# Chunk recurrences of the RWKV-7 branch: two quarters in one walk instead of two walks

## The chip, the cores and the metric

The kernel runs on one NeuronCore of a Trainium2 chip. Its engines run side by side, each through its own queue in order: PE (TensorE: matmuls; PEld is its weight loads), DVE (VectorE), ACT (ScalarE), POOL (GpSimd) and SP, whose queue here issues nearly all DMAs. The metric is the device time of one launch in microseconds (us). Before the change the median of three runs is 1436.8 us (1435.89 to 1438.96).

## What is computed

Two decoder layers over 256 positions of width 1024, all in fp32. In each layer one wide input projection feeds three token mixers: A, a gated linear recurrence; B, a dilated attention; C, RWKV-7. Their outputs are projected, gated, summed and projected again; a layer norm, a SwiGLU feed-forward part with a short convolution and a second layer norm follow. Branch C has 16 heads of 64 channels, each with a 64 x 64 state, and is the part that the change touches. Cut to its core:

```python
def step(st, inp):                     # one position, all heads
    r_t, w_t, k_t, v_t, kk_t, a_t = inp
    sa = jnp.einsum('bhij,bhj->bhi', st, -kk_t)
    st = (st * w_t[:, :, None, :] + sa[..., None] * (kk_t * a_t)[:, :, None, :]
          + v_t[..., None] * k_t[:, :, None, :])
    return st, jnp.einsum('bhij,bhj->bhi', st, r_t)
_, y = lax.scan(step, zeros, xs)
y = group_norm(y) * ln_w + ln_b
y_c = (y + bonus) * (sigmoid(zg) @ g2)          # g2: low-rank factor of the gate, 128 x 1024
merged = g_a * (y_a @ proj_a) + g_b * (y_b @ proj_b) + g_c * (y_c @ proj_c)
```

## The kernel before

**Dense work.** Activations lie feature by position (128 features in the partitions, 256 positions along). An fp32 weight tile is split into a high part `whi` (ACT or POOL) and a rest `wlo` (DVE or POOL), activations likewise (`hh`, `hl`); three matmuls in the fast fp32 format then stand for one fp32 product (`mm3`, line 818). These matmuls, with `whi` or `wlo` in the name, are called dense here; they are a fixed list of jobs in a fixed order (`ORDER`, line 69: `z0` to `z3` make the inputs of the four quarters of branch C, `q` those of branch B, `x`, `e` those of branch A, `g` the merge gates, `b`, `a`, `c` the three output projections).

**Branch C.** `branch_c(qt)` (line 993) handles a quarter, four heads: two tiles of 128 partitions (index `j`) with two heads each (index `p`). It first prepares: decay, key norms, products within chunks of 64 positions (`KR`, `BK`, `AL`, `AR`), the inverse of a triangular 64 x 64 matrix per head and chunk (`inverse`, line 969: 15 steps of two POOL instructions on `VS`, then small matmuls `DN,Om`, `xq,Om`, `X,AL`, `XT,W` that end in `XT`). Then it walks through four chunks in order (from line 1216). A chunk has three steps, with a copy out of PSUM between them: the residual `R` (matmuls `St,KR` and `UV,AL`), the solve (`R,XT`, copied into `UV`), and the next state `St` (`UV,KB`) with the output `Y` (`AR,UV` and `KR,St`). The tail squares `Y`, sums over heads with two matmuls (`shi,blk` and `slo,blk`), takes a reciprocal root, multiplies by the gate (`zg,g`, which needs `g2`) and leaves `yc`. `yc_split` (line 1564) splits it into `ych`, `ycl`, the input of the last output projection, job `c`. Quarter 2 begins after quarter 0 has ended, quarter 3 after quarter 1.

**What sets the order.** The program is laid out by a planner, class `Flow` (line 77), when it is built. The dense jobs are one stream; the quarters, the two other branches and the splits are side streams, Python generators that give up control at `yield`. The planner keeps its own clock for each engine, and at each moment issues the step of a side stream whose inputs are ready by that clock, or else the next dense step. On the chip each engine then runs its list in order and waits where an input is late. In `group` (line 849), used for the first jobs of `c`, the planner emits matmuls on a tile of zeros (`idle`) for as long as its clock has the next input not ready:

```python
while k >= warm and ((*need, k) not in fl.done or fl.done[(*need, k)] > fl.t["PE"]):
    if spare is None:
        spare = faux()[:, :S]
    T.matmul(spare, idle[:, :128], idle, start=True, stop=True)
    yield
```

**Fetches.** `fetch` (line 370) puts a DMA on SP's queue. Weight tiles go through a ring of four; SP waits for the oldest to be used up, and what stands behind it in the queue waits too.

Of the kernel before, what the change touches and what calls it, by code (L numbers as in the profile page):

```python
# [24 lines left out]
F32 = mybir.dt.float32  # L25
# [8 lines left out]
S = 256  # L34
# [33 lines left out]
COOL = 5000  # L68
ORDER = "z0 q z1 z2 z3 g10 x0 x1 g11 e0 e1 b0 g00 g01 g21 b1 a0 g20 a1 c".split()
NC = 2  # L70
NB, NUP = (16, 24), 8

# [246 lines left out]
def hybrid_kernel(ctx: ExitStack, tc: tile.TileContext, x, c, positions, mod_w, w_in, w_qkv, w_vres, lru, lora, g2w,  # L319
# [571 lines left out]
    def layer(l):  # L891
# [101 lines left out]
        def branch_c(qt):  # L993
            ident, epsc = K["ident"], K["epsc"]
            if qt >= 2:
                yield ("C", l, qt - 2)
            vfs = []
# [5 lines left out]
            wa2 = LR[l][:, S * qt:S * qt + S]  # L1003
            g2 = t1([128, S], "g2")
            fetch(g2, g2w[l, :, S * qt:S * qt + S])
            if l:
# [39 lines left out]
            r_ = E["r", qt]  # L1046
            ce = sb.tile([128, 2, 4], F32, name="ce", bufs=4)
            V.tensor_copy(ce, cum[:, :, :, 64])
# [167 lines left out]
            Y = s2([128, 2, S], "Y")  # L1216
            Sp = None

            def bank():
                return aux().rearrange("p (j i) -> p j i", j=8)[:, :2]  # L1220

            for c_ in range(4):
                ps = bank()
                for p in range(2):
                    o = rows(1 - p)
                    for j in range(2):
                        if c_:
                            T.matmul(ps[o, j], KR[j][rows(p), c_, 0], Sp[rows(p), j], start=True, stop=False)
                        T.matmul(ps[o, j], AL[p][rows(p), c_, j], UV[p][rows(p), c_, j], start=not c_, stop=True)
                fl.sync()  # L1230
                R = t1([128, 2, 64], "R")
                SC.activation(R, ps, AF.Copy, scale=-1.0)
                yield
                ps = bank()
                for p in range(2):
                    o = rows(1 - p)
                    for j in range(2):
                        T.matmul(ps[o, j], XT[o, 2 * c_ + j], R[o, j], start=True, stop=True)
                fl.sync()
                V.tensor_copy(UV[0][rows(1), c_], ps[rows(1)])  # L1240
                SC.activation(UV[1][rows(0), c_], ps[rows(0)], AF.Copy)
                yield
                if c_ < 3:
                    ps = bank()
                    for p in range(2):
                        for j in range(2):
                            T.matmul(ps[rows(p), j], KB[p][:, j, c_], UV[p][:, c_, j], start=True, stop=True)
                    Sn = t1([128, 2, 64], "St")
                    if c_:
                        V.tensor_tensor(Sn, Sp, ce[:, :, c_:c_ + 1].to_broadcast([128, 2, 64]), OP.mult)  # L1250
# [7 lines left out]
                for p in range(2):  # L1258
                    for j in range(2):
                        T.matmul(psy[rows(p), j], UV[p][:, c_, j], AR[p][:, c_, j], start=j == 0, stop=not c_,  # L1260
                                 skip_group_check=True)
                if c_:
                    for j in range(2):
                        for p in range(2):
                            T.matmul(psy[rows(p), j], Sp[rows(p), j], KR[j][rows(p), c_, 1], start=False, stop=True,
                                     skip_group_check=True)
# [4 lines left out]
                yield  # L1271

            sq = s2([128, 512], "sq")
# [488 lines left out]
        def spawn_c(qt):  # L1762
            fl.spawn(("C", l, qt), branch_c(qt), 1)

# [11 lines left out]
        loras()  # L1776
        for z in ORDER:
            at.setdefault(z, len(jobs))
# [22 lines left out]
        n4 = len(jobs)  # L1801
        spread([(l, n) for n in range(NB[l], 40)], n1, n4)
# [4 lines left out]
        hook(n2 - 6, spawn_a)  # L1807
        hook(n3, m0_done)
# [135 lines left out]
```

## Time and profile before

| | |
|---|---|
| median of three runs | 1436.8 us |
| the profiled execution: time, span of its instructions | 1436.41 us, 1434.7 us |
| mean granted clock of PE | 0.975 |
| PE busy | 1331.7 us, 93% |
| DVE busy | 1118.9 us, 78% |
| ACT busy | 844.5 us, 59% |
| POOL busy | 280.3 us, 20% |
| DMA queues, share of 16 engines | 52% |

Busy time is the sum over an engine's instructions with overlaps counted once. PE's matmuls overlap, so the time of one in the trace (0.28 us for a dense one) is longer than the distance from one start to the next, and it is the distance that counts. The mixers of layer 0 lie between 122 and 474 us, those of layer 1 between 748 and 1172 us; job `c` follows at once.

### The profile page before, as it was taken

What the parts mean: (1) busy time and instruction counts of PE and PEld (TensorE: products, weight loads), DVE (VectorE), ACT (ScalarE), POOL (GpSimd) and SP (SyncE); (2) the same over time, 40 slices, a digit from 0 to 9 for tenths busy, and PEclk for the clock granted to TensorE, in tenths of its full rate; (3) what the DMA queues carried; (4) which work ended last, traced back from release to release, by engine and by line L of the source; (5) the groups of instructions that cost most, each with busy time, mean ns of one, the idle gap of its engine ahead of it and who ended that gap; (6) DMA issues with size and microseconds to landing.
All of it is one profiled execution on the core that took longest, in us unless ns stands there. A gap on an engine that the chain in (4) does not pass through costs nothing.

```text
span 1434.7 us, 32557 instructions
## 1 busy us (share of the span) xinstructions
PE 1331.7 (93%) x12786; PEld 1256.9 (88%) x12786; DVE 1118.9 (78%) x2559; ACT 844.5 (59%) x1744; POOL 280.3 (20%) x454
## 2 busy tenths in 40 slices
PE   4699999998989999999998999899989899999996
PEld 3689988887889999998988998888879799999996
DVE  7688769767875878999968757887598758799964
ACT  3556657567765556665456557565767445567643
POOL 1304034302420021000031402453204000420001
PEclk9889999999989999999999999999999999999999
DMA  8546426342554755778945542444335447367662
GB/s 301 196 160 192 153 87 214 100 140 76 197 170 138 233 176 177 256 246 297 328 145 181 157 156 98 147 143 137 117 106 175 148 134 234 98 230 233 213 190 69
DMA packets 77613, 249.21 MB, mean 174 GB/s; under 512 B 8754, under 2 KB 12082, under 8 KB 77460
## 3 DMA queue, kind: packets, MB, share of 16 engines
q1 hardware_dynamic: 76660, 244.62, 51.5%
q0 software_dynamic: 800, 2.52, 0.5%
q8 instruction: 100, 1.64, 0.5%
q14 instruction: 53, 0.43, 0.1%
HBM read 243.96 MB, written 3.15 MB: 172 GB/s over the span
## 4 chain that ended last, share of the span: by engine, by line
PE 60%; DVE 23%; ACT 8%; DMA 5%; issue 4%; SPq 0%; DVEq 0%; ACTq 0%
PE mm L267 45%; PE aux L267 9%; DVE wlo L267 7%; PE faux L267 6%; DVE u L267 2%; DMA w<-in_mod_w_dram 2%; ACT whi L267 2%; DVE w L267 1%; DVE wc L267 1%; DMA w<-in_w_in_dram 1%; DVE BK L267 1%; ACT L267 1%; DVE fal L267 1%; DVE xc L267 1%; ACT kk L267 1%
## 5 line engine op out<-in xcount | busy, mean ns | idle before, releaser
L267 ACT ACTIVATE whi<-w 128x512 fp32r<-128x512 f32 (+1 forms) x647 | 370.1, 617 | 230.3 <-PE mm L267 67.1
L267 PE MATMUL mm<-hh,whi 128*128 128x256 f32 x1704 | 500.8, 294 | 0.5 <-ACT ge L267 0.5
L267 PE MATMUL mm<-hh,wlo 128*128 128x256 f32 x1704 | 484.2, 284 | 14.1 <-DVE wlo L267 13.6
L267 PE MATMUL mm<-hl,whi 128*128 128x256 f32 x1704 | 481.9, 283 | 0.0
L267 DVE TENSOR_TENSOR wlo<-w,whi 128x512 fp32r<-128x512 f32 (+1 forms) x644 | 434.2, 705 | 56.5 <-ACT whi L267 53.7
L267 PEld LDWEIGHTS mm<-hh,wlo 128*128 128x128 f32 x1704 | 322.8, 189 | 17.7 <-DVE wlo L267 17.0
L267 PEld LDWEIGHTS mm<-hh,whi 128*128 128x128 f32 x1704 | 322.8, 189 | 13.4 <-issue 4.6
L267 PEld LDWEIGHTS mm<-hl,whi 128*128 128x128 f32 x1704 | 323.2, 190 | 0.9
L267 POOL TENSOR_TENSOR wlo<-w,whi 128x512 fp32r<-128x512 f32 x60 | 87.2, 1459 | 306.5 <-ACT whi L267 235.1
L267 POOL TENSOR_SCALAR whi<-w 128x512 fp32r<-128x512 f32 x57 | 40.8, 721 | 411.7 <-PE mm L267 272.5
L267 PE MATMUL mm<-fal,whi 128*128 128x256 f32 x352 | 99.1, 281 | 1.3 <-DVE fal L267 1.3
L267 PE MATMUL mm<-fah,wlo 128*128 128x256 f32 x352 | 99.2, 282 | 0.9 <-DVE wlo L267 0.8
L267 PE MATMUL mm<-fah,whi 128*128 128x256 f32 x352 | 99.3, 282 | 0.1
L267 DVE SCALAR_TENSOR_TENSOR u<-mm,par,u 128x255 f32<-128x255 f32 (+1 forms) x172 | 82.2, 479 | 12.9 <-ACT u L267 9.6
L267 PE MATMUL mm<-whi,hh 128*128 128x256 f32 x288 | 85.3, 296 | 0.0
L267 PE MATMUL mm<-wlo,hh 128*128 128x256 f32 x288 | 83.6, 290 | 1.2 <-DVE wlo L267 1.2
L267 PE MATMUL mm<-whi,hl 128*128 128x256 f32 x288 | 83.2, 289 | 0.0
L267 DVE SCALAR_TENSOR_TENSOR w<-w,s_bc 128x512 f32<-128x512 f32 x96 | 68.5, 739 | 0.1
L267 PEld LDWEIGHTS mm<-fah,wlo 128*128 128x128 f32 x352 | 66.4, 189 | 1.6 <-DVE wlo L267 1.5
L267 PEld LDWEIGHTS mm<-fal,whi 128*128 128x128 f32 x352 | 66.1, 188 | 1.6 <-DVE fal L267 1.5
L267 PEld LDWEIGHTS mm<-fah,whi 128*128 128x128 f32 x352 | 66.2, 188 | 0.3 <-ACT fah L267 0.3
L267 ACT ACTIVATE u<-mm,par 128x256 f32<-128x256 f32 x86 | 47.5, 554 | 23.1 <-PE mm L267 23.0
(438 smaller groups left out, 2729.8 us busy)
## 6 DMA issues: line engine op xcount, KB each, us to landing
w<-in_w_in_dram SPq DMA_DIRECT2D x132, 512.0 KB, 3.5
w<-in_w_up_dram SPq DMA_DIRECT2D x88, 512.0 KB, 3.9
w<-in_mod_w_dram SPq DMA_DIRECT2D x64, 512.0 KB, 4.4
w<-in_w_qkv_dram SPq DMA_DIRECT2D x36, 512.0 KB, 4.1
wc<-in_mod_w_dram SPq DMA_DIRECT2D x64, 256.0 KB, 4.7
w<-in_w_dn_dram SPq DMA_DIRECT2D x32, 512.0 KB, 4.4
w<-in_w_pa_dram SPq DMA_DIRECT2D x16, 512.0 KB, 3.9
w<-in_w_pc_dram SPq DMA_DIRECT2D x16, 512.0 KB, 3.8
```

The source lines that it names most:

```text
L267: r = f(*a, **k)
```

## The change

- A quarter's stream, now named `prep`, ends when `XT` is there. A new stream, `recurrence(pr)`, waits for the preparation of quarters `2*pr` and `2*pr + 1` and walks through the chunks for both: each step issues the matmuls of both (index `z`) into one PSUM bank; `R` and `St` become twice as wide and are copied once, while the copies into `UV` and `Y` stay one per quarter.
- The tail becomes a stream of its own, one per quarter; both start when the joint walk has ended. It fetches `g2` itself; before, the fetch stood at the start of the preparation.
- Quarters 2 and 3 still begin after the tails of 0 and 1.
- `ORDER` is given per layer, and `LATER`, `EARLY_A` and `FOLLOW` are new settings; at their values they change nothing.

```diff
+            E["cp", qt] = KR, AL, AR, UV, KB, XT
+            E["tail", qt] = k_
+        def recurrence(pr):
+            for z in range(2):
+                yield ("prep", l, 2 * pr + z)
+            Z = [E.pop(("cp", 2 * pr + z)) for z in range(2)]
...
+            each = [(p, z, j) for p in range(2) for z in range(2) for j in range(2)]
             for c_ in range(4):
                 ps = bank()
-                for p in range(2):
+                for p, z, j in each:
+                    KR, AL, AR, UV, KB, XT = Z[z]
                     o = rows(1 - p)
-                    for j in range(2):
-                        if c_:
-                            T.matmul(ps[o, j], KR[j][rows(p), c_, 0], Sp[rows(p), j], start=True, stop=False)
-                        T.matmul(ps[o, j], AL[p][rows(p), c_, j], UV[p][rows(p), c_, j], start=not c_, stop=True)
+                    if c_:
+                        T.matmul(ps[o, z, j], KR[j][rows(p), c_, 0], Sp[rows(p), z, j], start=True, stop=False)
+                    T.matmul(ps[o, z, j], AL[p][rows(p), c_, j], UV[p][rows(p), c_, j], start=not c_, stop=True)
                 fl.sync()
-                R = t1([128, 2, 64], "R")
+                R = t1([128, 2, 2, 64], "R")
...
-                SC.activation(Y[:, :, 64 * c_:64 * c_ + 64], psy, AF.Copy)
+                for z in range(2):
+                    SC.activation(Ys[z][:, :, 64 * c_:64 * c_ + 64], psy[:, z], AF.Copy)
...
+            for z in range(2):
+                fl.spawn(("C", l, 2 * pr + z), tail(2 * pr + z, Ys[z]), 1)
+        def tail(qt, Y):
+            g2 = t1([128, S], "g2")
+            fetch(g2, g2w[l, :, S * qt:S * qt + S])
...
-            fl.spawn(("C", l, qt), branch_c(qt), 1)
+            fl.spawn(("prep", l, qt), branch_c(qt), 1)
+            if qt % 2:
+                fl.spawn(("rec", l, qt // 2), recurrence(qt // 2), 1)
```

PE, layer 0, the residual step of the second chunk before: the step of one quarter (its tiles end in 725, 726, 883, 884, 1016, 1017), with `p = 0` in the first four rows and `p = 1` in the next four.

```order
L267 MATMUL aux<-St,KR_725 64x64
L267 MATMUL aux<-UV_883,AL_1016 64x64
L267 MATMUL aux<-St,KR_726 64x64
L267 MATMUL aux<-UV_883,AL_1016 64x64
L267 MATMUL aux<-St,KR_725 64x64
L267 MATMUL aux<-UV_884,AL_1017 64x64
L267 MATMUL aux<-St,KR_726 64x64
L267 MATMUL aux<-UV_884,AL_1017 64x64
```

The same step now, of which the first ten of sixteen rows stand here (the second quarter's tiles are 1987, 1988, 2172, 2303):

```order
L270 MATMUL aux<-St,KR_721 64x64
L270 MATMUL aux<-UV_879,AL_1012 64x64
L270 MATMUL aux<-St,KR_722 64x64
L270 MATMUL aux<-UV_879,AL_1012 64x64
L270 MATMUL aux<-St,KR_1987 64x64
L270 MATMUL aux<-UV_2172,AL_2303 64x64
L270 MATMUL aux<-St,KR_1988 64x64
L270 MATMUL aux<-UV_2172,AL_2303 64x64
L270 MATMUL aux<-St,KR_721 64x64
L270 MATMUL aux<-UV_880,AL_1013 64x64
```

The matmuls of `p = 0` of both quarters now come first, then those of `p = 1`; their number is the same.

PE, layer 1, where job `c` begins (`ych`: a quarter's split output; one job of the first three after the other, before):

```order
L267 MATMUL mm<-yah,wlo 128x256
L267 MATMUL mm<-ych,whi 128x256
L267 MATMUL mm<-ycl,whi 128x256
L267 MATMUL mm<-ych,wlo 128x256
L267 MATMUL mm<-ych,whi 128x256
L267 MATMUL mm<-ycl,whi 128x256
L267 MATMUL mm<-ych,wlo 128x256
L267 MATMUL faux<-ych,whi 128x256
L267 MATMUL faux<-ycl,whi 128x256
```

The same job now, after the inputs from quarters 0 and 1 are used up (the last residual step of quarters 2 and 3, tiles 13486 to 13941, stands right in it):

```order
L270 MATMUL faux<-ych,wlo 128x256
...
L270 MATMUL aux<-St,KR_13486 64x64
L270 MATMUL aux<-UV_13826,AL_13941 64x64
L270 MATMUL aux<-St,KR_13487 64x64
L270 MATMUL aux<-UV_13826,AL_13941 64x64
L270 LDWEIGHTS idle
L270 MATMUL faux<-idle 128x256
...
L270 MATMUL aux<-R,XT 64x64 x8
```

From there to the next `ych` row PE has 102 matmuls on the tile of zeros, and between them the last solve, the last output step and both tails; before, the job has none. In the whole program these matmuls go from 286 to 388. In layer 0 the job has none before and none now.

SP, layer 1, around the fetches of `g2` (`g`) for quarters 2 and 3 now (`w`: weight tiles, of job `c` and of the projection after it):

```order
L375 DMA w_15376<-in_w_pc_dram 128x1024
L375 DMA w_15419<-in_w_pc_dram 128x1024
L375 DMA g_15582<-in_g2w_dram 128x256
L375 DMA g_15590<-in_g2w_dram 128x256
L375 DMA w_15755<-in_w_o_dram 128x1024
```

Before, quarter 3's fetch stands some 40 rows earlier, among the weights of the input projection, beside its fetches of `v_first`. The change leaves the other counts nearly as they are: DVE has 16 instructions less, ACT 13 less (5 of them table loads), POOL 12 less, SP as many.

## Rows read from the trace of the kernel before

**Rows 1.** Page, share of the span by engine: busy, and the chain that ended last.
```profile
PE 1331.7 (93%) x12786; PEld 1256.9 (88%) x12786; DVE 1118.9 (78%) x2559; ACT 844.5 (59%) x1744; POOL 280.3 (20%) x454
...
PE 60%; DVE 23%; ACT 8%; DMA 5%; issue 4%; SPq 0%; DVEq 0%; ACTq 0%
```
**Rows 2.** Chain of waits, 1150 to 1200 us: start, length, what.
```profile
1149.85 0.39 PE aux L267 x8
...
1181.17 2.72 PE mm L267 x23
```
**Rows 3.** Waits of PE, 748 to 1172 us: us in total, times, longest.
```profile
PE aux L267 <- DVE DN L267: 4.4, 1, 4.4
...
PE aux L267 <- DVE UV L267: 0.3, 1, 0.3
```
**Rows 4.** Waits of PE, 122 to 474 us.
```profile
PE aux L267 <- DVE X L267: 3.2, 1, 3.2
...
PE aux L267 <- DVE DN L267: 0.4, 1, 0.4
```
**Rows 5.** PE in order of time, 518 to 531 us: start, length, instruction, count.
```profile
519.93 4.32 PE L267 MATMUL faux<-idle 128*128 128x256 bf16 x38
524.09 0.60 PE L267 MATMUL aux<-lsum,ones_d 128*128 128x256 f32 x2
```
**Rows 6.** PE in order of time, 280 to 283 us.
```profile
280.50 0.29 PE L267 MATMUL mm<-hh,wlo 128*128 128x256 f32 x1
280.72 0.32 PE L267 MATMUL aux<-St,KR 64*64 64x64 f32 x2
...
281.00 0.33 PE L267 MATMUL aux<-St,KR 64*64 64x64 f32 x4
...
281.40 0.28 PE L267 MATMUL aux<-UV,AL 64*64 64x64 f32 x2
281.61 0.39 PE L267 MATMUL mm<-hh,whi 128*128 128x256 f32 x1
```
**Rows 7.** PE in order of time, 1155 to 1156 us.
```profile
1155.33 0.28 PE L267 MATMUL mm<-hh,wlo 128*128 128x256 f32 x1
1155.54 0.46 PE L267 MATMUL aux<-R,XT 64*64 64x64 f32 x8
1155.92 0.39 PE L267 MATMUL mm<-hh,whi 128*128 128x256 f32 x1
```
**Rows 8.** ACT in order of time, the end of quarter 3, layer 1.
```profile
1154.38 0.28 ACT L267 ACTIVATE R<-aux 128x128 f32<-128x128 f32 x1 [1.34 <-PE aux L267]
...
1158.38 0.63 ACT L267 ACTIVATE sq<-Y 128x512 f32<-128x512 f32 x1
```
**Rows 9.** DVE in order of time, the same stretch.
```profile
1159.71 0.69 DVE L267 TENSOR_TENSOR slo<-sq,shi 128x512 fp32r<-128x512 f32 x1 [0.95 <-ACT shi L267]
...
1166.62 0.48 DVE L267 SCALAR_TENSOR_TENSOR yc<-sq,par,aux 128x256 f32<-128x256 f32 x1
...
1168.86 0.68 DVE L267 TENSOR_TENSOR ycl<-yc,ych 128x512 fp32r<-128x512 f32 x1
```
**Rows 10.** PE in order of time: the gate's matmuls, and where job `c` begins.
```profile
1164.19 1.02 PE L267 MATMUL aux<-zg,g 128*128 128x256 f32 x4
...
1172.49 0.28 PE L267 MATMUL mm<-ych,whi 128*128 128x256 f32 x1
```
**Rows 11.** DMA issues: KB each, median us from issue to landing.
```profile
g<-in_g2w_dram SPq DMA_DIRECT2D x8, 128.0 KB, 3.4
```
**Rows 12.** Waits of SP's queue: us in total, times, longest.
```profile
SPq L372 <- DVE wlo L267: 885.3, 282, 22.1
```
**Rows 13.** POOL in order of time: first and last row of quarter 3's inverse, layer 1.
```profile
1088.87 0.53 POOL L267 TENSOR_TENSOR itmp<-VS,N 128x15 f32<-128x15 f32 x1 [0.66 <-DVE N L267]
...
1114.31 0.23 POOL L267 TENSOR_TENSOR VS<-VS,itmp 128x8 f32<-128x8 f32 x1
```
**Rows 14.** PE in order of time, 1114 to 1123 us.
```profile
1122.59 1.08 PE L267 MATMUL aux<-DN,Om 32*32 32x32 f32 x64 [4.35 <-DVE DN L267]
```

More of the change, by code (lines that the diff above doesn't have):

```diff
@@ L68 @@
 COOL = 5000
-ORDER = "z0 q z1 z2 z3 g10 x0 x1 g11 e0 e1 b0 g00 g01 g21 b1 a0 g20 a1 c".split()
+ORDER = ["z0 q z1 z2 z3 g10 x0 x1 g11 e0 e1 b0 g00 g01 g21 b1 a0 g20 a1 c".split()] * 2
+LATER = ((0, 0), (0, 0))
+EARLY_A = (6, 6)
 NC = 2
+FOLLOW = "C"
 NB, NUP = (16, 24), 8
@@ L1046, in branch_c @@
             r_ = E["r", qt]
-            ce = sb.tile([128, 2, 4], F32, name="ce", bufs=4)
+            if qt % 2 == 0:
+                E["ce", qt // 2] = sb.tile([128, 2, 2, 4], F32, name="ce", bufs=4)
+            ce = E["ce", qt // 2][:, qt % 2]
             V.tensor_copy(ce, cum[:, :, :, 64])
@@ L1215, in branch_c @@
                 SC.activation(XT[r0:r0 + 32, :, 32:64], ps[r0:r0 + 32, :8], AF.Copy, scale=-1.0)
-            Y = s2([128, 2, S], "Y")
+            E["cp", qt] = KR, AL, AR, UV, KB, XT
[4 more added lines that the diff above has]
+            Z = [E.pop(("cp", 2 * pr + z)) for z in range(2)]
+            ce = E.pop(("ce", pr))
+            Ys = [s2([128, 2, S], "Y") for _ in range(2)]
             Sp = None
             def bank():
-                return aux().rearrange("p (j i) -> p j i", j=8)[:, :2]
+                return aux().rearrange("p (z j i) -> p z j i", z=4, j=2)[:, :2]
+            each = [(p, z, j) for p in range(2) for z in range(2) for j in range(2)]
             for c_ in range(4):
                 ps = bank()
-                for p in range(2):
+                for p, z, j in each:
+                    KR, AL, AR, UV, KB, XT = Z[z]
                     o = rows(1 - p)
-                    for j in range(2):
-                        if c_:
-                            T.matmul(ps[o, j], KR[j][rows(p), c_, 0], Sp[rows(p), j], start=True, stop=False)
-                        T.matmul(ps[o, j], AL[p][rows(p), c_, j], UV[p][rows(p), c_, j], start=not c_, stop=True)
+                    if c_:
+                        T.matmul(ps[o, z, j], KR[j][rows(p), c_, 0], Sp[rows(p), z, j], start=True, stop=False)
+                    T.matmul(ps[o, z, j], AL[p][rows(p), c_, j], UV[p][rows(p), c_, j], start=not c_, stop=True)
                 fl.sync()
-                R = t1([128, 2, 64], "R")
+                R = t1([128, 2, 2, 64], "R")
                 SC.activation(R, ps, AF.Copy, scale=-1.0)
@@ L1234, in branch_c @@
                 ps = bank()
-                for p in range(2):
+                for p, z, j in each:
                     o = rows(1 - p)
-                    for j in range(2):
-                        T.matmul(ps[o, j], XT[o, 2 * c_ + j], R[o, j], start=True, stop=True)
+                    T.matmul(ps[o, z, j], Z[z][5][o, 2 * c_ + j], R[o, z, j], start=True, stop=True)
                 fl.sync()
-                V.tensor_copy(UV[0][rows(1), c_], ps[rows(1)])
-                SC.activation(UV[1][rows(0), c_], ps[rows(0)], AF.Copy)
+                for z in range(2):
+                    UV = Z[z][3]
+                    V.tensor_copy(UV[0][rows(1), c_], ps[rows(1), z])
+                    SC.activation(UV[1][rows(0), c_], ps[rows(0), z], AF.Copy)
                 yield
@@ L1244, in branch_c @@
                     ps = bank()
[L1245 to L1248, printed above, removed]
+                    for p, z, j in each:
+                        UV, KB = Z[z][3:5]
+                        T.matmul(ps[rows(p), z, j], KB[p][:, j, c_], UV[p][:, c_, j], start=True, stop=True)
+                    Sn = t1([128, 2, 2, 64], "St")
                     if c_:
-                        V.tensor_tensor(Sn, Sp, ce[:, :, c_:c_ + 1].to_broadcast([128, 2, 64]), OP.mult)
+                        V.tensor_tensor(Sn, Sp, ce[:, :, :, c_:c_ + 1].to_broadcast([128, 2, 2, 64]), OP.mult)
                         fl.sync()
@@ L1257, in branch_c @@
                 psy = bank()
[L1258 to L1261, printed above, removed]
+                for p, z, j in each:
+                    UV, AR = Z[z][3], Z[z][2]
+                    T.matmul(psy[rows(p), z, j], UV[p][:, c_, j], AR[p][:, c_, j], start=z == j == 0, stop=not c_,
+                             skip_group_check=True)
                 if c_:
[L1263 to L1266, printed above, removed]
+                    for z in range(2):
+                        for j in range(2):
+                            for p in range(2):
+                                T.matmul(psy[rows(p), z, j], Sp[rows(p), z, j], Z[z][0][j][rows(p), c_, 1], start=False,
+                                         stop=True, skip_group_check=True)
                 fl.sync()
-                SC.activation(Y[:, :, 64 * c_:64 * c_ + 64], psy, AF.Copy)
+                for z in range(2):
+                    SC.activation(Ys[z][:, :, 64 * c_:64 * c_ + 64], psy[:, z], AF.Copy)
                 if c_ < 3:
@@ L1271, in branch_c @@
                 yield
+            for z in range(2):
+                fl.spawn(("C", l, 2 * pr + z), tail(2 * pr + z, Ys[z]), 1)
+        def tail(qt, Y):
+            epsc = K["epsc"]
+            k_ = E.pop(("tail", qt))
+            g2 = t1([128, S], "g2")
+            fetch(g2, g2w[l, :, S * qt:S * qt + S])
             sq = s2([128, 512], "sq")
@@ L1776, in layer @@
         loras()
-        for z in ORDER:
+        for z in ORDER[l]:
             at.setdefault(z, len(jobs))
@@ L1801, in layer @@
         n4 = len(jobs)
-        spread([(l, n) for n in range(NB[l], 40)], n1, n4)
+        spread([(l, n) for n in range(NB[l], 40)], n1 + LATER[l][0], n4 - LATER[l][1])
         load = out_proj()
@@ L1806, in layer @@
         hook(n1, spawn_b)
-        hook(n2 - 6, spawn_a)
+        hook(n2 - EARLY_A[l], spawn_a)
         hook(n3, m0_done)
```

4 lines of the change are left out of this document (1 added, 3 removed).

## The prediction

> **What bounds the kernel now.** I read the page first, then the chain of waits, the waits of PE in the two stretches of the mixers, and PE's instructions one by one where branch C's steps stand between dense matmuls. PE is busy for 93% of the span and holds 60% of the chain that ended last [rows 1]. Where branch C ends in layer 1 the chain is PE alone, matmul after matmul, from 1149.85 to 1183.9 us [rows 2]: whatever is put into PE's queue there moves the end by its own length. So the question is what the change adds to and takes from PE's list, and which waits of PE come or go.
>
> **The added idle matmuls.** The list of after has 102 more matmuls on the tile of zeros than before, all in job `c` of layer 1, before the inputs from quarters 2 and 3. They wait for nothing, so they take their time whether the inputs are early or late. 38 such matmuls in a row last from 519.93 to the next start at 524.09 us [rows 5]: 4.16 / 38 = 0.109 us each, and 102 x 0.109 = **+11.1 us**. Why they are there can be read from the order: before, quarter 2 of layer 1 began some 600 dense matmuls ahead of quarter 3 and was through long before job `c`; now both begin side by side, about where quarter 3 began, and share ACT, DVE and POOL up to the end. In layer 0 the last gate matmuls (`zg,g`) stand 61 rows of PE's list before the first of job `c`, against 64 before, and nothing is added.
>
> **The steps themselves.** The number of recurrence matmuls is unchanged; what changes is how they are packed. A residual step of one quarter: last dense start 280.50, first start of the step 280.72, of its second half (`p = 1`) 281.00, last start 281.40 in a row of two, so about 281.46, next dense 281.61 [rows 6]. A dense matmul takes 0.12 us from start to start, so going in costs 0.22 - 0.12 = 0.10 us and coming out about 0.15 - 0.06 = 0.09 us: 0.19 us for each interruption. Each matmul is two passes, and within one half they start 0.058 us apart (eight passes of the second half, 281.00 to 281.46). The first half would last 8 x 0.058 = 0.46 us, and the second begins 0.28 us after it: the halves overlap by three passes, 0.18 us.
>
> Doubled, the first half has 16 passes. If the overlap stays three passes, the second half starts after 13 x 0.058 = 0.75 us and ends 0.93 us later: 1.68 us, against 2 x (0.28 + 0.46) = 1.48 us: +0.20 us. The solve is the other case: all of it lies between 1155.33 and 1155.92 us [rows 7], 0.59 - 0.12 - 0.19 = 0.28 us, its halves of four passes nearly side by side; doubled, each half has eight as in rows 6, so 0.74 against 0.56: +0.18 us. I use +0.19 for all steps where the halves stand one behind the other. They are 15 in a joint walk (residual 4, solve 4, state 3, output 4), 60 in four walks: 60 x 0.19 = +11.4 us. Against that, the 96 steps of eight quarters become 48, and if each had interrupted the dense stream by itself, 48 x 0.19 = -9.1 us would be saved. But part of them shared an interruption already: by my count of the two lists the dense stream is interrupted 192 times in the two mixers before, 174 times after. But where steps shared one, a change of the tile's shape between them is saved, which costs about as much. I take both at two thirds, +7.6 - 6.1 = **+1.5 us**; the ends are -9 (no overlap lost) and +11 (nothing saved).
>
> The Trainium skill (TensorEngine Tiling (Array Packing), Key Properties) says that tiles operate independently and different ones can load weights and multiply in parallel. By that rule alone the halves would always run side by side; rows 6 show 0.28 us of delay in a step of eight passes a half, so here it holds for the last passes only. It gives one of the rivals below.
>
> **What leaves the other engines.** Sixteen ACT and sixteen DVE instructions and five table loads less, and some POOL work that the planner deals out anew. PE's work covers them all; where an engine in front of PE is late it shows in the waits below. I count nothing.
>
> **The end of both tails.** Before, the last walk takes from `R` at 1154.38 us [rows 8] to `ycl`, 1168.86 + 0.68 = 1169.5 us [rows 9]: 15.2 us, and the job that reads it starts at 1172.49 [rows 10], so 3 us before it would be needed. Now a second tail runs in the same stretch. On DVE, which is the slower of the two, that is 0.69 (`slo`), about as much for the product, 4 x 0.48 and 0.68 [rows 9]: about 4 us, to 19 us; on ACT five instructions of 0.63 as `sq` [rows 8] lie beside it. In PE's list the stretch from the last residual step on has 11.1 us of idle matmuls and some 4 us of the steps and sums (a solve 0.9, an output step 1.4, the sums and gates about 1.7, by the rows above), 15 us, and two more us are given by quarter 2's share of job `c`. So up to 19 - 17 = 2 us of real wait could stand behind the idle matmuls; less, since DVE has no dense work to prepare while PE idles. **+0.5 us**, between 0 and +4.
>
> **The fetch of `g2`.** It stood long before its use; now it is issued when the tail starts and read by `zg,g` at the tail's end, which is 1164.19 - 1158.38 = 5.8 us later in the walk of before [rows 8, 10]. It takes 3.4 us to land [rows 11], and two go one after the other. But SP's queue runs in order and waits a mean of 885.3 / 282 = 3.1 us for a weight tile's buffer [rows 12]; if the fetch stands behind such a wait it lands after 6.5 to 7 us, and PE, which takes `zg,g` in order, stops with all dense work behind it. The second tail lengthens the time until use by a few us. **+0.5 us**, between 0 and +5 (four pairs at a bit over 1 us).
>
> **The other waits.** PE waits for branch C's pieces (rows with `aux`) 8.8 us in layer 1 (eight rows, from 4.4 to 0.3) [rows 3] and 12.1 us in layer 0 (ten rows, from 3.2 to 0.4) [rows 4]. All of these places stand elsewhere in the new list. Half could vanish as well as half be added: 0, between -10 and +10.
>
> **Sum.** 11.1 + 1.5 + 0.5 + 0.5 = +13.6 on the profiled execution's 1436.41 us: 1450.0. The profiled execution lies 0.4 us under the median of the runs, which I leave. I trust the first term most and the packing least, and of the two ways in which the waits can go I see slightly more on the good side (half the walks, half the places to be late at), so I set **1448 us**, +11.6.
>
> **Rivals.**
> - *More waits at the inverses* (chance 0.15). Quarter 3's inverse in layer 1 took from 1088.87 to 1114.54 us on POOL among other work [rows 13], and PE then stood 4.35 us before `DN,Om` [rows 14]. Now two inverses of the second pair run at once in both layers, 60 instructions on the same queue. If PE stands that long at each of the four `DN,Om`, it is three more stops, 3 x 4.35 = 13 us: 1448 + 13 = 1461. Against it: the list puts these matmuls later than before, too.
> - *The walk's waits vanish and pay for the idle matmuls* (0.15). Half of the 20.9 us of `aux` waits gone is -10.4: 1438, no change.
> - *Faster* (0.10). The joint walk has half the round trips PE -> ACT -> PE, and with one walk instead of two there are fewer moments at which PE reaches a step before its copy. If nearly all `aux` waits vanish, -20.9, the result is 1448 - 20.9 = 1427. It turns faster from about 14 of the 21 us on. Against it: the largest of them, `DN` and `X`, stand before the walk, in the preparation.
> - *The halves overlap fully* (0.04). Then a doubled step lasts 0.93 us instead of 1.68, and the solve 0.46 instead of 0.74: about 0.3 us for the short ones and 0.75 for the 12 long residual steps, 48 x 0.28 + 12 x 0.75 = 22 us less: 1426. Rows 6 speak against it, and it is the rule named above.
>
> **Chances and range.** The forecast (1441 to 1456) has 0.56; with the first rival, slower is 0.71. No change (within 0.2%, 2.9 us, what a measurement of this kernel can tell) has 0.15, faster 0.14. The range reaches up into the first rival and down through no change: 1434 to 1460.
>
> **What will show it.** In the new profile: 388 idle matmuls, 102 of them in one stretch near 1170 us, about 11 us long, with little or no wait behind them; residual steps of about 1.9 us from dense to dense for two quarters; `zg,g` rows without a DMA as releaser. Wrong would be: PE reaching job `c` of layer 1 more than 5 us earlier than 1172.5 us (then waits did vanish), or more than 5 us later (then the second pair's preparation stopped it); or a solve step of two quarters well under 0.9 us.

## The result and the profile after

| | before | after |
|---|---|---|
| median, runs on one chip | 1436.35 us (1431.03 to 1438.96) | 1452.59 us (1449.85 to 1455.8) |
| profiled execution, span | 1436.41 us, 1434.7 us | 1455.8 us, 1454.1 us |
| mean granted clock of PE | 0.975 | 0.97 |

The change makes the kernel slower: ratio 1.0119, 95% interval [1.0083, 1.0155], +16 us. The forecast was 1448 us. The profiled execution of after lies 3.2 us above its median and has the lowest mean clock of the four: 0.970, where the other three have 0.976 and 0.977.

The page's busy times and chain, which answer to [rows 1]:

```profile
PE 1350.5 (93%) x12888; PEld 1282.8 (88%) x12888; DVE 1109.4 (76%) x2543; ACT 843.2 (58%) x1731; POOL 266.0 (18%) x442
...
PE 58%; DVE 21%; ACT 10%; DMA 6%; issue 4%; SPq 0%; POOL 0%; DVEq 0%; ACTq 0%
```

PE has its 102 matmuls more, DVE and ACT less work, and the share of ACT in the chain has grown. One place where ACT stands in it now and did not before [rows 2] is the end of the second pair in layer 1. PE in order of time there (start, length, instruction, count):

```profile
1172.81 0.28 PE L270 MATMUL faux<-ych,wlo 128*128 128x256 f32 x1
1173.02 0.32 PE L270 MATMUL aux<-St,KR 64*64 64x64 f32 x2
1173.18 0.28 PE L270 MATMUL aux<-UV,AL 64*64 64x64 f32 x2
1173.30 0.28 PE L270 MATMUL aux<-St,KR 64*64 64x64 f32 x2
...
1174.84 2.03 PE L270 MATMUL faux<-idle 128*128 128x256 bf16 x17
1176.80 0.96 PE L270 MATMUL aux<-R,XT 64*64 64x64 f32 x16
...
1178.57 0.97 PE L270 MATMUL aux<-AR,UV 128*64 128x64 f32 x16
...
1187.59 3.88 PE L270 MATMUL faux<-idle 128*128 128x256 bf16 x34
1191.22 0.36 PE L270 MATMUL mm<-ych,whi 128*128 128x256 f32 x1
1191.69 0.39 PE L270 MATMUL mm<-ycl,whi 128*128 128x256 f32 x1
```

The first row is a matmul of job `c`: PE reached this job at 1165.29 us, 7 us earlier than before [rows 10], because steps that stood ahead of it before now stand in it (about 10 us of small matmuls) and because PE waited 4.2 us less on the way there through layer 1. From 1174.84 to 1191.22 us, 16.4 us, there is no dense work: 11.1 us of matmuls on zeros (102 at 0.109 us) and 5.3 us of the last steps, sums and gates. What ended that stretch is told by the chain of waits (start, length, what):

```profile
1174.91 1.96 PE faux L270 x17
1176.87 0.89 PE aux L270 x16
1177.77 0.87 PE faux L270 x7
1178.64 1.53 PE aux L270 x32
1180.19 0.45 ACT Y L270 x2
...
1183.01 1.28 ACT L354
...
1190.55 0.48 DVE yc L270
1191.03 0.61 DVE ycl L270
1191.64 0.04 issue
1191.69 0.86 PE mm L270 x5
```

From 1180.19 us on it is the two tails, ACT and then DVE, and not PE's list as in [rows 2]. Ahead of that PE's list is in the chain: the 24 idle matmuls (`faux`) on both sides of the last solve hold it up for 2.8 us. The last `R` of the walk is copied at 1174.95 us, where before it was 1154.38 [rows 8]; from there to the last `ycl` it is 17.5 us, against 15.2.

Busy times in two stretches, of before and then of after (columns: stretch, its length, busy time and instructions of PE, PEld, DVE, ACT, POOL, mean granted clock of PE, DMA share, GB/s):

```profile
122.00:266.00 144.00, 135.73 (x1571) 125.56 (x1571) 115.00 (x297) 91.85 (x201) 39.43 (x75) 0.96 0.47 154
266.00:360.00 94.00, 86.51 (x1005) 77.84 (x1005) 66.52 (x140) 60.50 (x127) 13.28 (x26) 0.98 0.33 107
```
```profile
122.00:266.00 144.00, 141.46 (x1733) 132.99 (x1731) 102.38 (x259) 84.64 (x194) 32.92 (x53) 1.00 0.48 158
266.00:360.00 94.00, 76.53 (x525) 70.13 (x523) 76.27 (x158) 65.37 (x123) 17.77 (x22) 0.87 0.33 111
```

In layer 0 after is first ahead, then loses more than it gained: while the first pair's tails and the second pair's preparation run, PE is idle for 17.5 us of 94 (7.5 before) and the clock granted is 0.87 in the mean: 2.4 GHz but for five pieces at 1.2 GHz, 23.9 us together, each of which begins in or right behind a stop of PE of 1.1 to 2.6 us. What PE waits for there in after (us in total, times, longest):

```profile
PE mm L270 <- DVE wlo L270: 5.5, 3, 2.6
PE aux L270 <- DVE yc L270: 3.1, 2, 1.6
PE aux L270 <- ACT shi L270: 2.8, 2, 1.6
PE mm L270 <- ACT whi L270: 2.2, 1, 2.2
```

In before the same stretch has 4.6 us on `wlo` and nothing else over 0.6.

**Where the 16 us are.** I count from start to start on PE, between dense matmuls that both kernels have (those with `ehi` and `elo` in the name, of job `e`, counted in; the 500th to the 2420th are layer 0's mixers, S0; the 4300th to the 6690th layer 1's mixers and job `c`, S1). S0 goes from 371.7 to 379.6 us: waits +4.5, dense matmuls at the lower clock +3.1, the rest +0.3. S1 goes from 446.4 to 456.2: idle matmuls +11.1, small matmuls +3.5, waits -4.1, lower clock +2.4, and the dense matmuls -3.1, which stays unexplained. After S1 the profiled execution loses 4.5 more and between the mixers 0.9; it had started 3.7 us ahead. Together that is its +19.4.

Of layer 0's part the waits come back and the clock does not. The lists of PE in layer 0 are the same in after and in three of the kernels below (no_idle, rec_l1, g2_early). Their S0 is 377.0 to 378.2 us, with waits of 27.2 to 28.2 us against 22.1 before, and the lower clock costs their dense matmuls no more than in before (7.3 to 7.5 us each, 10.6 in after): in the second stretch above their mean clock is 0.92 to 0.95, but in the first 1.00, where before has 0.98 and 0.96. So the 3.1 us of clock belong to this one execution; a loss of 5 to 8 us, with waits of 4.5 to 6, is what the change does to layer 0.

### The profile page after: what moved, and what is told of

Read it like the earlier page. It is cut to its first block, busy times and chain, and to the rows that moved or that the text cites. A ratio compares the mean times of both kernels' runs of the same rounds, so it can differ in the third digit from the quotient of the medians.

```text
span 1454.1 us, 32738 instructions
## 1 busy us (share of the span) xinstructions
PE 1350.5 (93%) x12888; PEld 1282.8 (88%) x12888; DVE 1109.4 (76%) x2543; ACT 843.2 (58%) x1731; POOL 266.0 (18%) x442
## 4 chain that ended last, share of the span: by engine, by line
PE 58%; DVE 21%; ACT 10%; DMA 6%; issue 4%; SPq 0%; POOL 0%; DVEq 0%; ACTq 0%
PE mm L270 43%; PE aux L270 9%; DVE wlo L270 7%; PE faux L270 6%; ACT whi L270 2%; DVE u L270 2%; DMA w<-in_w_in_dram 2%; DMA w<-in_mod_w_dram 2%; DVE wc L270 1%; DVE w L270 1%; DVE BK L270 1%; ACT L270 1%; DVE xc L270 1%; DVE sq L270 1%; ACT kk L270 1%
## 5 line engine op out<-in xcount | busy, mean ns | idle before, releaser
L270 ACT ACTIVATE whi<-w 128x512 fp32r<-128x512 f32 (+2 forms) x655 | 374.0, 616 | 221.6 <-PE mm L270 65.9
L270 PE MATMUL mm<-hl,whi 128*128 128x256 f32 x1704 | 487.0, 286 | 0.0
L270 DVE TENSOR_TENSOR wlo<-w,whi 128x512 fp32r<-128x512 f32 (+1 forms) x648 | 435.8, 704 | 59.7 <-ACT whi L270 58.3
L270 PEld LDWEIGHTS mm<-hh,wlo 128*128 128x128 f32 x1704 | 330.9, 194 | 19.1 <-DVE wlo L270 18.7
L270 PEld LDWEIGHTS mm<-hh,whi 128*128 128x128 f32 x1704 | 331.6, 195 | 17.0 <-issue 6.7
L270 PEld LDWEIGHTS mm<-hl,whi 128*128 128x128 f32 x1704 | 331.5, 195 | 1.2
L270 POOL TENSOR_TENSOR wlo<-w,whi 128x512 fp32r<-128x512 f32 x56 | 77.8, 1397 | 307.9 <-ACT whi L270 187.7
L270 POOL TENSOR_SCALAR whi<-w 128x512 fp32r<-128x512 f32 x49 | 34.3, 707 | 475.3 <-PE mm L270 354.6
```

The costliest lines, as they stand in the source:

```text
L270: r = f(*a, **k)
```

## The experiments

The table has what the trace of each kernel gives by the same count; the medians of before were 1435.6, 1436.9 and 1437.1 us beside them. "Small" is all non-dense, non-idle matmuls of S0 and S1, "waits" PE's gaps there, "idle" the matmuls on zeros in job `c`. "Walk" is the part of "small" that the walk's own matmuls take, with time in stretches at 1.2 GHz counted half: an estimate of their price at full clock, from the granted clock of each trace. Every row is one execution, so "small" and S0, S1 also hold what the clock did in it; "walk" is 68.9 to 69.1 us in all five kernels whose joint walk goes in blocks.

| kernel | median us | ratio to before, 95% interval | S0 | S1 | small | walk | waits | idle |
|---|---|---|---|---|---|---|---|---|
| before | 1436.4 | | 371.7 | 446.4 | 205.9 | 67.0 | 51.3 | 0 |
| after | 1452.6 | 1.0119 [1.0083, 1.0155] | 379.6 | 456.2 | 209.8 | 69.0 | 51.7 | 11.1 |
| no_idle | 1452.2 | 1.0105 [1.0075, 1.0135] | 378.2 | 456.2 | 213.7 | 69.1 | 61.7 | 0 |
| rec_l1 | 1457.7 | 1.0138 [1.0106, 1.0170] | 377.0 | 462.5 | 211.6 | 68.9 | 62.2 | 0 |
| b_coupled | 1439.3 | 1.0022 [1.0000, 1.0043] | 371.3 | 449.9 | 208.4 | 66.1 | 43.3 | 12.4 |
| pair_split | 1446.0 | 1.0060 [1.0040, 1.0080] | 374.9 | 453.6 | 198.4 | 58.8 | 63.8 | 0 |
| stagger | 1445.8 | 1.0060 [1.0040, 1.0080] | 372.8 | 453.8 | 202.1 | 69.0 | 46.5 | 13.6 |
| g2_early | 1455.3 | 1.0132 [1.0096, 1.0169] | 377.7 | 461.2 | 208.3 | 68.9 | 57.0 | 8.3 |
| b_p_inner | 1424.0 | 0.9905 [0.9878, 0.9932] | 368.9 | 438.3 | 195.9 | 58.7 | 46.2 | 0 |
| p_inner | 1419.5 | 0.9872 [0.9840, 0.9904] | 362.7 | 440.8 | 189.2 | 49.7 | 46.7 | 5.0 |
| b_p_inner2 | 1408.8 | 0.9796 [0.9769, 0.9824] | 361.2 | 426.4 | 191.9 | 61.2 | 42.8 | 0 |
| p_inner2 | 1410.1 | 0.9814 [0.9779, 0.9848] | 357.4 | 435.8 | 181.5 | 49.6 | 45.5 | 5.0 |
| p2_stagger | 1416.3 | 0.9864 [0.9822, 0.9907] | 360.1 | 436.7 | 177.1 | 49.5 | 46.1 | 11.4 |
| ps2 | 1434.0 | 0.9985 [0.9966, 1.0004] | 361.4 | 452.1 | 188.6 | 53.2 | 49.5 | 16.3 |

**1. Are the idle matmuls the price? (no_idle)** In `group` the planner waits for the input of `c` where it put idle matmuls:

```diff
-                while k >= warm and (... fl.done[(*need, k)] > fl.t["PE"]):
+                if need[0] == "yck" and (... fl.done[(*need, k)] > fl.t["PE"]):
+                    yield (*need, k)
+                while need[0] != "yck" and k >= warm and (...):
```

> The changed kernel without its 102 idle matmuls in job c of layer 1; the planner waits there instead. Theory A (the end of branch C is late and the idle matmuls only fill the time until then): the time stays at 1452 us (1449 to 1456); PE stands about 11 us before the rows of quarter 2's input, which are ready near 1191 us in the trace of the changed kernel. Theory B (the idle matmuls cost their own length, as the prediction has it): 1452.6 - 11.1 = 1441.5 us.

The time is that of after, as theory A has it. PE now waits, as its rows in order of time show (idle time and releaser in brackets):

```profile
1179.67 0.80 PE L270 MATMUL aux<-shi,blk 128*128 128x512 f32 x1 [1.72 <-ACT shi L270]
...
1186.93 0.38 PE L270 MATMUL mm<-ych,whi 128*128 128x256 f32 x1 [1.21 <-ACT ych L270]
...
1189.48 0.58 PE L270 MATMUL mm<-ycl,whi 128*128 128x256 f32 x1 [2.17 <-DVE ycl L270]
```

From 1174 to 1186 us the granted clock is 0.57 here and 1.00 in the same place of after: PE, which stands still in between, falls to 1.2 GHz, its small matmuls take up to twice as long (16 `AR,UV` 1.76 us for 0.97), and still the end is no later. From the copy of `Y` to the end of the chain in `ycl` ACT and DVE take 11.45 us in both traces (1177.99 to 1189.44 us here, 1180.19 to 1191.64 in after; the chain's rows here follow). Ahead of it the 2.8 us of idle matmuls in the chain are gone, but the slower matmuls take all but 0.6 us of them back. So most of the idle matmuls fill a stretch that the late tails make, and taking them out wins nothing. Two things change together here, the matmuls on zeros and the clock; no run separates them.

```profile
1177.99 0.45 ACT Y L270 x2
...
1188.83 0.61 DVE ycl L270
1189.44 0.04 issue
```

**2. What does the pairing of starts and ends cost by itself? (b_coupled)** Before, with its separate walks; in layer 1 quarters 2 and 3 both wait for both of the first pair (and two buffers are dealt out otherwise, 24 and 45 for 21 and 46, so that it fits).

```diff
                 yield ("C", l, qt - 2)
+                if l:
+                    yield ("C", l, 3 - qt)
```

> The kernel before the change, every quarter with a walk of its own, but in layer 1 quarters 2 and 3 both wait until both of the first pair have ended (two pool sizes changed to make room: 24 small buffers for 21, 45 large for 46). PE's list has 113 idle matmuls in job c of layer 1. Theory A (starting as a pair is what makes the end late): 12 to 16 us over the kernel before, 1448 to 1453 us. Theory B (walking together is what costs): within 3 us of the kernel before, 1434 to 1440 us.

It has 12.4 us of idle matmuls in job `c` (113, where after has 102) and costs 3 us (0 to 6 by the interval), the time of theory B: the waits elsewhere in layer 1 went down by 7.8 us. The wait for `DN` [rows 14] is among those gone, as it is in after. A late end in layer 1 is therefore no loss of its full length.

**3. The second pair earlier (rec_l1).** After, where in layer 1 the second pair begins when the first joint walk has ended, not the tails.

```diff
-                yield (FOLLOW, l, 0) if FOLLOW == "rec" else (FOLLOW, l, qt - 2)
+                yield ("rec", l, 0) if l else ("C", l, qt - 2)
```

> The changed kernel, but in layer 1 quarters 2 and 3 begin when the joint walk of the first pair has ended, not after its tails. PE's list then has 286 idle matmuls as before the change, none of them in job c. Theory A (what costs in layer 1 is that the second pair starts late, as a pair): the stretch of idle matmuls goes, 11 to 16 us less, 1437 to 1442 us, and the 4 to 5 us lost in layer 0 stay. Theory B (the joint walk itself costs): little change, 1448 us or more.

No idle matmul is left in job `c`, and the kernel is no faster than after. Theory A missed by more than 15 us; theory B's bound of 1448 held, though not its "little change": the median is 5 us above after's, with intervals that overlap. PE's waits rose to 62 us; the longest new one, 4.1 us, is for `slo` of a tail. I take it that work moved earlier to relieve the end came to lie beside the first pair's tails; no run shows that apart.

**4. The steps without sharing (pair_split).** After's pairing, but a bank, an `R` and an `St` for each quarter, one quarter's matmuls after the other's.

```diff
-                ps = bank()
-                for p, z, j in each:
+                for z in range(2):
+                    ps = bank()
+                    for p, j in each:
...
-                SC.activation(R, ps, AF.Copy, scale=-1.0)
+                    SC.activation(R[z], pss[z], AF.Copy, scale=-1.0)
```

> The changed kernel with its pairing kept (both preparations first, the two quarters step by step in one stream, both tails after it, the next pair after the tails), but each quarter with banks, R and St of its own as before the change. PE's list has no idle matmuls in job c. Theory A (the pairing costs: two tails and two preparations fall together, the dense work's wlo comes late and PE's clock falls): near the changed kernel, 1446 to 1455 us. Theory B (the shared banks and double-width copies cost): back near the kernel before, 1435 to 1441 us.

Its small matmuls take 198.4 us, 7.5 less than before and 11.4 less than after; the walk at full clock takes 8.3 less than before and 10.2 less than after. A residual step of two quarters costs 1.557 us beyond a dense matmul (1.916 in after), a solve 0.749 (0.982). These are the two opposite terms of the packing: pairing saves the entry and exit, and joint steps with the halves in blocks lose the overlap. The edit changes banks, copies and order at once; what the order does alone, experiment 5 shows. The time, 1446.0 us, is at the lower edge of theory A's range all the same: what the steps and the missing idle matmuls save is taken back by 12.1 us more of waits and by the lowest granted clock of all these kernels (0.966 in the trace).

**5. Halves in turn (b_p_inner, p_inner).** The loops are turned round, so that matmuls of `p = 0` and `p = 1` alternate; nothing else changes. In before (b_p_inner; the solve, state and output likewise) and in after (p_inner):

```diff
-                for p in range(2):
-                    o = rows(1 - p)
-                    for j in range(2):
+                for j in range(2):
+                    for p in range(2):
+                        o = rows(1 - p)
```
```diff
-            each = [(p, z, j) for p in range(2) for z in range(2) for j in range(2)]
+            each = [(p, z, j) for z in range(2) for j in range(2) for p in range(2)]
```

> The kernel before the change with the two halves (p) of a step issued in turn, matmul by matmul, instead of one half after the other. Theory A (the array runs the halves side by side whenever the list lets it, so what the prediction priced at 0.28 us of delay per step is a matter of the order): a residual step falls from 1.11 us dense to dense to about 0.85, the other steps by 0 to 0.2; 8 x (3 x 0.28 + 8 x 0.1) = 13 us at most on PE's list, of which waits take some back: 1423 to 1432 us. Theory B (the array takes the second half late whatever the order): no change, 1434 to 1439 us.

> The changed kernel with the halves (p) of a step issued in turn. In the kernel before, this took a residual step from 0.98 to 0.75 us beyond the dense matmul; doubled steps have twice as many passes to lay side by side: residual 1.92 to about 1.2, solve 0.98 to 0.75, state and output 2.17 to about 1.7. Per joint walk 3 x 0.7 + 4 x 0.23 + 4 x 0.45 = 4.8 us, four walks 19 us. Theory A (these are PE time on the chain): 1452.6 - 19 = 1433 us (1428 to 1438), and steps of these lengths. Theory B (doubled steps overlap no better): 1448 to 1453 us.

Both became faster than before, b_p_inner as its theory A has it, p_inner 8.5 us below the range of its theory A (1428 to 1438). The residual step in p_inner, in order of time; in after it is the first group of rows above:

```profile
426.90 0.28 PE L270 MATMUL mm<-yah,wlo 128*128 128x256 f32 x1
427.11 0.34 PE L270 MATMUL aux<-St,KR 64*64 64x64 f32 x4
427.27 0.29 PE L270 MATMUL aux<-UV,AL 64*64 64x64 f32 x4
427.39 0.33 PE L270 MATMUL aux<-St,KR 64*64 64x64 f32 x4
...
427.97 0.33 PE L270 MATMUL aux<-UV,AL 64*64 64x64 f32 x4
428.23 0.39 PE L270 MATMUL mm<-yah,whi 128*128 128x256 f32 x1
```

From the dense matmul ahead to the matmul behind it is 1.33 us instead of 2.03 in after (1172.81 to 1174.84). Rows of four now start 0.12 us apart, where in after rows of two do: the halves run side by side. For one quarter, in b_p_inner, it is 0.87 us from 972.76 us to 973.63 instead of 1.11 [rows 6]:

```profile
972.76 0.28 PE L267 MATMUL mm<-hh,wlo 128*128 128x256 f32 x1
972.97 0.34 PE L267 MATMUL aux<-St,KR 64*64 64x64 f32 x4
...
973.63 0.39 PE L267 MATMUL mm<-hh,whi 128*128 128x256 f32 x1
```

The small matmuls give 20.6 of p_inner's 33 us; by steps it is 0.70 x 12 residuals, 0.28 x 16 solves, 0.39 x 12 states with output, and 1.1 each for the four last outputs and the four first residuals, 19.8; the walk at full clock gives 19.2. The rest is mainly waits (-5.0) and idle matmuls (-6.1), which I put down to the shorter steps; no run separates them.

Put side by side, the four kernels show what joining two walks is worth: with the halves in blocks it costs 1.9 us of walk (67.0 to 69.0), with the halves in turn it saves 9.0 (58.7 to 49.7).

**6. Two tails at once? (stagger)** After, the second tail of a pair begins when the first has ended.

```diff
-            for z in range(2):
-                fl.spawn(("C", l, 2 * pr + z), tail(2 * pr + z, Ys[z]), 1)
+            def after_first():
+                yield ("C", l, 2 * pr)
+                yield from tail(2 * pr + 1, Ys[1])
+            fl.spawn(("C", l, 2 * pr), tail(2 * pr, Ys[0]), 1)
+            fl.spawn(("C", l, 2 * pr + 1), after_first(), 1)
```

> The changed kernel, but the second tail of a pair starts when the first has ended. PE's list has 125 idle matmuls in job c instead of 102. Theory A (two tails at once are what makes wlo late and the clock fall behind them): the waits before dense matmuls behind the tails in both layers (about 7 us in layer 0 near 310 to 330 us, 10 us in layer 1 near 1014 to 1037 us in the trace of the changed kernel) shrink to half, against 2 to 3 us for the later end: 1444 to 1450 us. Theory B (the tails side by side are not it): those waits stay and the end is later, 1452 to 1457 us.

6.7 us of the 16 are gone, which is theory A's time, but not by its mechanism. PE's waits for the dense weights `wlo` and `whi` did not shrink to half: over layer 0 they are 11.8 us (7.7 in after), over layer 1 8.4 (9.8). By the traces the small matmuls take 7.7 us less and all waits together 5.2 less, against 2.5 more of idle matmuls; but the walk takes 69.0 us as in after, and some 5 of the 7.7 us are time that the small matmuls spend longer at 1.2 GHz in the trace of after. In the stretch from 266 to 360 us PE is busy for 76.7 us as in after, so two tails at once are not shown to be what stops it there.

**7. The fetch of `g2` (g2_early).** After, the factor loaded at the start of the preparation as before, into two buffers of its own (pools 22 and 45).

```diff
+            E["g2", qt] = g2 = sb.tile([128, S], F32, name="g2", bufs=2)
+            fetch(g2, g2w[l, :, S * qt:S * qt + S])
...
-            g2 = t1([128, S], "g2")
-            fetch(g2, g2w[l, :, S * qt:S * qt + S])
+            g2 = E.pop(("g2", qt))
```

> The kernel after with the low-rank gate factor loaded where the mixer begins, as before the change, into two buffers of its own kind. Theory A (its load lands some 15 us ahead of its use also at the end, so moving it costs nothing): 1450 to 1455 us, the same as after. Theory B (SP's queue or the rings delay it at a tail): 1446 to 1449 us. The place of the end of job c is the same number of idle matmuls or fewer in either.

No gain: 1455.3 us, within the runs of after. In after SP issues the last two fetches 18 us before `zg,g` starts at 1185.64 us:

```profile
1167.78 0.90 SPq L375 DMA_DIRECT2D g<-in_g2w_dram  x2
```

**8. The same order in the inverse (b_p_inner2, p_inner2).** Two sets of small matmuls of the inverse (`X,AL` and `XT,W`) alternate their halves too, in before with separate walks and in after with joint ones:

```diff
-            for p in range(2):
-                r0 = 64 * (1 - p)
-                for u in range(8):
+            for u in range(8):
+                for p in range(2):
+                    r0 = 64 * (1 - p)
```

> The kernel before with the halves issued in turn in the walk, and in the last two sets of small matmuls of the inverse (X,AL and XT,W) as well. By the trace of the kernel before those two sets take 248 starts at 0.029 us each, 7.2 us, twice; if the two halves then lie side by side, up to half of 14 us goes: theory A, 1424 - 5 = 1419 us (1415 to 1423). Theory B (starts in 32 x 32 tiles are limited by issue, not by the tile): 1423 to 1427 us, as with the walk alone.

> The kernel after with the halves in turn in the joint walk and in the two sets of the inverse. Theory A (the order of the halves is a price of its own, whatever walks together, so gains add): the inverse in turn was worth 15 us with separate walks (1424.0 to 1408.8), so 1419.5 - 15 = 1404 us. Theory B (in the joint form the late end of job c takes it back, since 78 idle matmuls stand there and not 46): 1408 to 1414 us, no better than the separate walks in this order.

b_p_inner2 is 6 us better than its theory A allowed; p_inner2 has the time of theory B. These are the two best kernels, and no difference between them can be told. (The idle matmuls of job `c` are 46 in both p_inner and p_inner2; the expectation's 78 was wrong.) The joint walk is 10.4 us cheaper in small matmuls (181.5 against 191.9), and by the two traces gives it back in layer 1: 5.0 us of idle matmuls, 7.2 us of dense matmuls (about what they spend longer at the lower clock), 1.7 us of waits. The clock's part is uncertain: the trace of b_p_inner2 is of its fastest execution, 4.7 us under its median and with the highest granted clock (0.985; the others 0.979 to 0.984).

**9. What is left of the pairing, in the better order (p2_stagger, ps2).** p_inner2 with the edit of stagger, and with the edit of pair_split (each quarter its own bank and copies, halves in turn).

> The kernel p_inner2 with the second tail of a pair after the first. Theory A (two tails together crowd VectorE and ScalarE, whatever the order of the matmuls): 6.7 us less than p_inner2 again, about 1397 to 1400 us. Theory B (with shorter steps there is room for both tails, and at the end of layer 1 the second tail comes later): the same as p_inner2 within 2 us, or up to 4 us more.

> The kernel p_inner2 with a bank, a residual and a state for each quarter, so pairing without sharing. Theory A (sharing cost 6 to 7 us in the kernel after only because the halves stood one after the other in longer pieces; in turn it saves the entry and exit of a step, 0.24 to 0.39 us for each of some 60 steps, some 12 to 17 us): 1413 to 1421 us, more than p_inner2. Theory B (shared banks and copies couple two quarters and cost 6 to 7 us in any order): 1397 to 1399 us, less than p_inner2.

The stagger that saved 6.7 us costs 6.1 now, in layer 0 and after job `c`, also more than theory B said. With separate banks the kernel is 24 us slower, more than either theory said. 7.1 us of that are small matmuls (3.6 us of walk at full clock); the largest part is 11.3 us of idle matmuls more (16.3 against 5.0), since the second pair's walk lands with three chunks inside job `c`, with nothing dense left to run beside it. A chunk then takes 7.2 us on its own, here from one residual step to the next (PE in order of time):

```profile
1148.97 0.34 PE L270 MATMUL aux<-St,KR 64*64 64x64 f32 x4
...
1150.10 0.83 PE L270 MATMUL faux<-idle 128*128 128x256 bf16 x6
1150.86 0.68 PE L270 MATMUL aux<-R,XT 64*64 64x64 f32 x16
...
1154.66 1.59 PE L270 MATMUL faux<-idle 128*128 128x256 bf16 x13
1156.18 0.34 PE L270 MATMUL aux<-St,KR 64*64 64x64 f32 x4
```

Where the walk lands in the order was worth more here than the steps themselves, and the time of ps2 is no clean measure of sharing.

## Why the prediction was right, and where its steps were not

The sign, the total (1448 against 1452.6 us) and the place of the largest term came out. That the total came so near is in part luck: the largest term is not a price of its own, two terms of the packing were both too small and cancel, and waits put at nothing rose in one layer by what they fell in the other.

- **Idle matmuls, +11.1.** Count, place and length are as predicted: 102, job `c` of layer 1, 11.1 us, and a wait of 0.4 us behind them. The reason was wrong in one sentence: "they take their time whether the inputs are early or late". The inputs were late: all but 2.8 us of the idle matmuls stand beside a chain that runs through the tails, and without them nothing is won (no_idle). What they stand for is the late end of a pair that runs side by side, and even that is no fixed price: b_coupled with 12.4 us of them loses only 3 us, since waits elsewhere fall. So 11.1 us as an addend to the sum came true beside other changes in layer 1, of which waits of -4.1 us are the largest.
- **Packing, +1.5.** The two terms, +7.6 and -6.1, measured +11.4 and -7.5 as the clock was granted (pair_split against after and before), so +3.9; the walk's matmuls alone, at full clock, give +10.2 and -8.3, so +1.9. The net was right; both terms were too small by a quarter, and these errors cancel. The overlap of three passes held: the residual step costs 1.92 us beyond a dense matmul, as my 1.68 and 0.19 say, 1.87 (from dense to dense it is 2.03, which I gave as 1.9); the solve costs 0.98, and one "well under 0.9" would have spoken against it.
- **Tails, +0.5.** The stretch from the last `R` to `ycl` is 17.5 us (I had said up to 19), and 0.4 us of real wait are left.
- **`g2`, +0.5.** It is 0. The fetch stands 18 us ahead, because the last residual, solve and output lie between, and the load takes 3.8 us at the median in after (3.4 before [rows 11]).
- **Other engines, 0.** I counted 16 instructions and five table loads off ACT; the page has 13 less in all. No term rests on it.
- **Other waits, 0.** The `aux` rows do come out level (6.5 us after 8.8 in layer 1, 11.9 after 12.1 in layer 0). The wait for `DN` is gone, and the first rival with it; of the inverse's stops layer 1 has none left, layer 0 still 1.7 us on `X` and 0.8 on `W`. But layer 0, which I had put at nothing since its job `c` has no idle matmuls, lost 5 to 8 us in the four executions of its list. This is the missing term: I had priced the waits for branch C's pieces, not those of the dense matmuls behind them, where `wlo` and `whi` go from 4.6 to 7.7 us (9.0 in no_idle). All waits together are +4.5 us in layer 0 and -4.1 in layer 1, so the 0 was right only as a sum. The clock behind PE's stops cost 5.5 us of dense matmuls in the profiled execution; that it costs anything in the median is not shown, since the other runs of after have no lower mean clock than before.
- **A sign of being wrong came.** PE reached job `c` of layer 1 7.2 us earlier than before, where more than 5 was to mean that waits vanished. Some did (4.2 us), so part of the second rival came true; the rest are steps that moved into the job.
- **Rival "the halves overlap fully"** (0.04, 1426 us). It did not come for this change. But it is a matter of order: p_inner, the same walk with the halves alternating, is at 1419.5 us, 33 us under after, of which 19.2 us are the walk (I had priced the rival at 22). I read rows 6 as a property of the chip, where it was one of the list. The Trainium skill (TensorEngine Tiling (Array Packing), Key Properties) says that tiles operate independently; where the list alternates between tiles the trace agrees (four small matmuls start in each 0.12 us, where there were two), and where it gives one tile a long run first, the other tile's matmuls stay behind it but for the last passes [rows 6].

What stays open: why layer 0 stops more between 266 and 360 us; stagger stops as long there, and p_inner2 waits 11.0 us for `wlo` in about the same place. Open, too, is how the 16 us divide between the late end in layer 1 and the waits in layer 0: no run takes one away and leaves the rest as it was. Medians of kernels that differ mainly in where steps land move by 5 to 7 us (rec_l1, stagger, p2_stagger), up and down, so single terms of that size are not settled by one pair of them.

## What to carry to other kernels

Matmuls that use different parts of the array should alternate in the list: joining two groups of them in blocks lengthens the run that the other part waits behind, and eats what the joining saves (here +1.9 us of walk in blocks, -9.0 in turn). Matmuls on zeros that a planner puts in place of a wait show where it holds an input to be late, so take them as a sign and ask the chain what ends there. Work in step ends in step: what two streams spread over time before, their tails and the last wait of the phase, comes at one moment, and where a step lands can be worth more than its own length (ps2).

## Hardware behaviour not expected

The order of the same small matmuls, as the only edit, took before from 1436.9 to 1408.8 us (the planner lays out the rest anew around them). In turn, a residual step costs about 0.28 us beyond its passes whether it is short or long: one quarter costs 0.75 us with eight passes a half, two quarters 1.22 with sixteen, at 0.058 us a pass. PE's granted clock was 0.57 of 2.4 GHz in the mean from 1174 to 1186 us, where PE stood still between its steps (no_idle), and 1.00 in the same stretch filled with matmuls on zeros (after).
